# Keeping a third quarter of the expert activations on chip, running the top-k search denser, and loading the gates in smaller pieces behind the weights

## The chip, the cores and the metric

One Trainium2 chip, one core. The metric is device time in microseconds (us) of one execution. The kernel's instructions are spread over TensorE (PE; its weight loads are PEld), VectorE (DVE), ScalarE (ACT), GpSimd (POOL) and SyncE (SP). SP and ACT also issue the transfers between DRAM and SBUF, the on-chip memory; each has its own queue of them (q1 and q10 in the profile).

## The reference, cut to what matters

Two transformer blocks run one after the other on 256 tokens of width 1024. The part that the change touches is the last one, a mixture of 16384 experts (128 x 128) called `peer`. For each token and each of 8 heads, 128 scores on each of two sides give the 16 best of each side, the 16 best of their sums give 16 experts, and a softmax over those gives their gates:

```
s = einsum('thpd,hpnd->thpn', q, sub_keys)
sv, si = top_k(s, 16)
top_v, top_i = top_k(sv0 + sv1 (all pairs), 16);  g = softmax(top_v)
a = gelu(einsum('td,thkd->thk', x, u[experts]))
out = einsum('thk,thkd->td', g * a, v[experts])
```

The kernel does not gather experts. It computes the products with all 16384 rows of `u`, multiplies by a matrix of gates that is zero nearly everywhere, and multiplies that by all of `v`.

## The kernel before, in words

All matrix products are done in about fp32 accuracy: each operand is split in a high and a low part, and each product is three matmuls. `Weights` (L139) brings weights in by tiles `raw` of 128 x 2048 (1 MB, L154, three buffers, issued on SP), and splits each half tile into `whi` (ACT, L133) and `wlo` (DVE, L130), three buffers of each. PE reads only the split halves.

**The u pass** (`u_pass`, L1042). Four quarters q of 32 blocks j; one step takes two blocks, so 16 steps a quarter and 64 in all. A step needs one `raw` tile, does 48 matmuls (L171 to L173) into one PSUM bank and has one Gelu on ACT (L1049). Quarters 0 and 1 go to SBUF tiles `ga[0]` and `ga[1]` and stay. Quarters 2 and 3 go to a ring of four tiles `gr`, and from there to DRAM (`ga_d`, L1051, queue of ACT).

**The side work.** While the u pass runs, a generator makes the gates: first `topk_steps` (L904, 44 pieces; most are the search on DVE; the two halves of the tokens, tt = 0 and 1, each end in transposes on PE, L976), then `g_steps` (L983, 33 pieces). Piece i of the latter builds one-hot matrices for 8 tokens on DVE (L999 to L1002), and does 16 small matmuls of the piece before (L1012), moves their result to a tile `gs` (ACT, L1014) and writes that to DRAM, 512 KB (`gg_d`, L1015, queue of ACT). `feed(n)` (L1029) advances the generator by n pieces on average: one per call in the eight calls of the search's score stage (L898), then 1.2 per step of the u pass while j is below 60 and 1.7 after (L1052). Transposes and gate matmuls are pinned by `issue_after` behind the last matmul traced so far on PE.

**The v pass** (`v_pass`, L1065). Again 64 steps of two blocks, 16 a quarter. A step takes the activations g (from `ga`, or for quarters 2 and 3 read back from DRAM, L1076, queue of SP), multiplies them in place by the gates `gh` (DVE, L1078), splits the product (`wgh` on ACT, `wgl` on DVE, two buffers of each) and does 48/2 = 24 matmuls of 512 columns (L1091). `gh` holds 16 blocks (HJ), 2 MB, two buffers; it is read from `gg_d` in runs of 512 bytes (16 blocks x 8 tokens x 4 bytes) by L1071 on SP's queue, eight times in all.

The order of instructions on each engine and each queue is not the order of the text. A planner lays it down when the kernel is built, from times that it estimates: an instruction that it takes to be ready may come far ahead of its place in the text, if nothing pins it. On the chip each engine then follows its own list in order and waits at each instruction for its operands. The weight loads, the gate loads and the read-backs are all on SP's list.

Of the kernel before, what the change touches and what calls it, by code (L numbers as in the profile page):

```python
# [10 lines left out]
F32 = mybir.dt.float32  # L11
# [5 lines left out]
AF = mybir.ActivationFunctionType  # L17
# [3 lines left out]
P = 128  # L21
S = 256
# [17 lines left out]
NE = NKEYS  # L40
# [23 lines left out]
def block_kernel(ctx: ExitStack, tc: tile.TileContext, a: dict, out: bass.AP, dbg=None):  # L64
    nc = tc.nc

    def pool(stack, name, bufs=1):
        return stack.enter_context(tc.tile_pool(name=name, bufs=bufs, reuse_waits="tile"))
# [8 lines left out]
    def bank(tag, name):  # L77
        return psum.tile([P, 512], F32, tag=tag, bufs=2, name=name)
# [5 lines left out]
    def ps_a(name="psa"):  # L84
        return bank("a", name)

    def ps_b(name="psb"):
        return bank("b", name)

    def ps_c(name="psc"):  # L90
        return bank("c", name)
# [26 lines left out]
    class Lo:  # L118
# [3 lines left out]
        def next(self):  # L122
            self.at += 1
            return self.cycle[self.at % len(self.cycle)]
# [7 lines left out]
    def split(dst_h, dst_l, src, eng="v"):  # L132
        nc.scalar.activation(dst_h, src, AF.Copy)  # L133
        sub(eng, dst_l, src, dst_h)

    last_load = [None]
# [31 lines left out]
    def mm3(ps, w, b, K, xs):  # L168
        for k in range(K):
            wh, wl = w(b + k)  # L170
            nc.tensor.matmul(ps, wh, xs[0][:, k], start=(k == 0), stop=False)  # L171
            nc.tensor.matmul(ps, wh, xs[1][:, k], start=False, stop=False)  # L172
            last_mm[0] = nc.tensor.matmul(ps, wl, xs[0][:, k], start=False, stop=(k == K - 1))  # L173
# [525 lines left out]
    with tc.high_priority():  # L699
# [7 lines left out]
        t = small.tile([P, 2], F32, name="yf2")  # L707
# [95 lines left out]
    for g in range(4):  # L803
        ps = ps_a()
# [46 lines left out]


    QJ = 32
    TG = 8
    NG = S // TG
    big = pool(ctx, "big")
    ga = [big.tile([P, QJ, S], F32, name=f"ga{q}") for q in range(2)]

    ring = pool(ctx, "ring", 4)
    dram = ctx.enter_context(tc.tile_pool(name="dram", bufs=1, space=bass.MemoryType.DRAM))  # L860
    ga_d = [dram.tile([P, QJ // 2, 2 * S], F32, name=f"gad{q}") for q in range(2)]
    gg_d = dram.tile([P, NG, NE * TG], F32, name="ggd")

    idxT = big.tile([P, 2, S], F16, name="idxT")
    gT = big.tile([P, 2, S], F16, name="gT")
# [117 lines left out]
    def g_steps():  # L983

        gp = pool(stg, "gp", 3)
        todo = None
        for i in range(NG + 1):
            new = None
            if i < NG:
                ts = slice(i * TG, (i + 1) * TG)  # L990

                def two(x):
                    return x.rearrange("p (g t) -> p g t", t=2)[:, :, None, :].to_broadcast([P, TG // 2, P, 2])

                io = iota2[:, None].to_broadcast([P, TG // 2, P, 2])
                o1 = gp.tile([P, TG // 2, P, 2], F16, tag="o1", name="o1")
                o2 = gp.tile([P, TG // 2, P, 2], F16, tag="o2", bufs=2, name="o2")
                og = gp.tile([P, 2, TG // 2, P, 2], F16, tag="og", name="og")
                nc.vector.tensor_tensor(o1, io, two(idxT[:, 0, ts]), op=OP.is_equal)  # L999
                nc.vector.tensor_tensor(o2, io, two(idxT[:, 1, ts]), op=OP.is_equal)  # L1000
                for c in range(2):
                    nc.vector.tensor_tensor(og[:, c], o2, two(gT[:, c, ts]), op=OP.mult)  # L1002
                new = i, o1, og
            if todo:
                i_, o1, og = todo
                gs = gp.tile([P, NE, TG], F32, tag="gs", bufs=2, name="gs")
                with tc.issue_after(last_mm[0].ins):
                    for g4 in range(TG // 4):
                        ps = (ps_d, ps_b)[g4]()
                        for t4 in range(4):  # L1010
                            for c in (1, 0):
                                nc.tensor.matmul(ps[:, t4 * P:(t4 + 1) * P], o1[:, 2 * g4 + t4 // 2, :, t4 % 2], og[:, c, 2 * g4 + t4 // 2, :, t4 % 2],  # L1012
                                                 start=(c == 1), stop=(c == 0))
                        nc.scalar.activation(gs[:, :, g4 * 4:g4 * 4 + 4], ps.rearrange("p (t j) -> p j t", t=4), AF.Copy)  # L1014
                nc.scalar.dma_start(gg_d[:, i_], gs.rearrange("p j t -> p (j t)"))  # L1015
            todo = new
            yield

# [2 lines left out]
    def side():  # L1021
        yield from topk_steps()
        st4.close()
        yield from g_steps()
# [4 lines left out]
    def feed(n):  # L1029
        due[0] += n  # L1030
        while due[0] >= 1.0:
            due[0] -= 1.0
            next(side_it, None)
# [8 lines left out]
    def u_pass(q):  # L1042
        w = Weights(a["uT"][:, q * QJ * D:(q + 1) * QJ * D])
        for j in range(0, QJ, 2):
            ps = ps_c()
            for i in range(2):
                mm3(ps[:, i * S:(i + 1) * S], w, (j + i) * KD, KD, h2)
            g = ga[q][:, j:j + 2] if q < 2 else ring.tile([P, 2, S], F32, tag="gr", name="gr")
            nc.scalar.activation(g, ps.rearrange("p (j t) -> p j t", j=2), AF.Gelu)  # L1049
            if q >= 2:  # L1050
                nc.scalar.dma_start(ga_d[q - 2][:, j // 2], g.rearrange("p j t -> p (j t)"))  # L1051
            feed(1.2 if q * QJ + j < 60 else 1.7)  # L1052

    for q in range(4):
        u_pass(q)
    for _ in side_it:
        pass
    stg.close()

    hot = pool(ctx, "hot", 2)  # L1060
    acc = [[ps_a("acc0"), ps_a("acc1")], [ps_b("acc2"), ps_b("acc3")]]

    HJ = 16

    def v_pass(q):  # L1065
        w = Weights(a["v"][:, q * QJ * D:(q + 1) * QJ * D])
        for j in range(0, QJ, 2):
            jj = q * QJ + j
            if j % HJ == 0:
                gh = hot.tile([P, NG, HJ, TG], F32, tag="gh", name="gh")  # L1070
                nc.sync.dma_start(gh, gg_d.rearrange("p g (j t) -> p g j t", t=TG)[:, :, jj:jj + HJ])  # L1071
            if q < 2:
                g = ga[q][:, j:j + 2]
            else:
                g = ring.tile([P, 2, S], F32, tag="gr", name="gr")
                nc.sync.dma_start(g.rearrange("p j t -> p (j t)"), ga_d[q - 2][:, j // 2])  # L1076
            gv = g.rearrange("p j (g t) -> p j g t", t=TG)
            nc.vector.tensor_tensor(gv, gv, gh[:, :, j % HJ:j % HJ + 2].rearrange("p g j t -> p j g t"), op=OP.mult)  # L1078
            wh = hot.tile([P, 2, S], F32R, tag="wgh", name="wgh")
            wl = hot.tile([P, 2, S], F32R, tag="wgl", name="wgl")  # L1080
            split(wh, wl, g)
            end = jj + 2 == NE
            hls = [w((j + i) * KD, KD) for i in range(2)]

            def block(i, tt, ns):
                hi, lo = hls[i]
                first, last = jj + i == 0, jj + i == NE - 1
                th, tl = wh[:, i, tt * P:(tt + 1) * P], wl[:, i, tt * P:(tt + 1) * P]
                for x_, w_, st, sp in ((th, hi, first, False), (th, lo, False, False), (tl, hi, False, last)):
                    for n in ns:  # L1090
                        r = nc.tensor.matmul(acc[tt][n], x_, w_[:, n * 512:(n + 1) * 512], start=st, stop=sp)  # L1091
                return r

            if not end:
                for i, tt in itertools.product(range(2), range(2)):
                    block(i, tt, range(2))
            else:

                r = None
                for tt, n in itertools.product(range(2), range(2)):  # L1100
                    with tc.issue_after(r.ins) if r else nullcontext():
                        for i in range(2):
                            r = block(i, tt, (n,))

    v_pass(0)
    v_pass(1)


# [140 lines left out]
def build(arrays, dbg=None):  # L1249
    import concourse.bacc as bacc  # L1250

    nc = bacc.Bacc("TRN2", target_bir_lowering=False, num_devices=1)
    aps = {n: nc.dram_tensor(f"in_{n}", v.shape, mybir.dt.from_np(v.dtype), kind="ExternalInput").ap()
           for n, v in arrays.items()}
    out = nc.dram_tensor("out_0", (S, D), F32, kind="ExternalOutput").ap()
    taps = None
    if dbg:
        taps = {n: nc.dram_tensor("dbg_" + n, s, F32, kind="ExternalOutput").ap() for n, s in dbg.items()}
    with tile.TileContext(nc, schedule_with_timeline_sim=True) as tc:
        block_kernel(tc, aps, out, taps)  # L1260
    return nc
# [9 lines left out]
```

## Time and profile before

| | us |
|---|---|
| median of 3 runs | 1413.62 (1412.87 to 1416.95) |
| profiled execution, its own time | 1420.62 |
| its span | 1418.8 |
| PE busy | 1375.2 |
| PEld / DVE / ACT / POOL busy | 1270.8 / 1013.1 / 704.9 / 23.8 |

The page is read from the top: busy time of each engine, then the span in 40 slices (35.5 us each) with the clock that TensorE was granted and what the DMA engines moved, then the chain of work that ended last. The queries on the trace used here are the windows (busy time of each engine in a stretch), the waits (who waited for whom), the timeline of one engine, and the view of one line or one tile. In that trace the u pass runs from 636 to about 1057 us and the v pass from there to about 1405 us.

### The profile page before, as it was taken

How to read it: one execution, taken by the hardware profiler on the slowest of the kernel's cores; microseconds unless marked ns; L12 is line 12 of the kernel's file. 1: busy time of each engine (PE TensorE's matmuls, PEld its weight loads, DVE VectorE, ACT ScalarE, POOL GpSimd, SP SyncE). 2: the span in 40 equal slices, each digit the busy share in tenths (PEclk: the TensorE clock that was granted, in tenths of full speed). 3: DMA queues.
4: the chain of work that ended last, by engine and by line, in shares of the span. 5: the costliest groups of instructions: out<-in, count | busy, mean ns of one | idle time of the engine just before them, and what ended most of it. 6: DMA issues, size and time to landing. Idle time of an engine off the chain costs nothing.

```text
span 1418.8 us, 24208 instructions
## 1 busy us (share of the span) xinstructions
PE 1375.2 (97%) x9776; PEld 1270.8 (90%) x9776; DVE 1013.1 (71%) x1749; ACT 704.9 (50%) x1030; POOL 23.8 (2%) x25
## 2 busy tenths in 40 slices
PE   7999999999999999899999999998999999999997
PEld 6967998999999888899999999998888888888885
DVE  6774777998888646699984489876536555566775
ACT  4443654454546555545454456554344454444443
POOL 1000000000000001000000000000000000000000
PEclk9998999999999999999999999999899999999999
DMA  6452456777795632444555578889975555588762
GB/s 239 154 196 82 141 169 234 269 279 267 262 328 191 218 125 72 152 170 158 187 198 180 178 257 311 296 296 321 340 287 197 190 197 199 198 300 289 262 233 86
DMA packets 88448, 308.86 MB, mean 218 GB/s; under 512 B 6416, under 2 KB 39824, under 8 KB 61200
## 3 DMA queue, kind: packets, MB, share of 16 engines
q1 hardware_dynamic: 78544, 279.26, 57.0%
q10 hardware_dynamic: 9792, 28.05, 5.0%
q8 instruction: 76, 1.25, 0.3%
q14 instruction: 36, 0.29, 0.1%
HBM read 281.08 MB, written 26.21 MB: 217 GB/s over the span
## 4 chain that ended last, share of the span: by engine, by line
PE 88%; DVE 5%; DMA 4%; issue 1%; ACT 1%; POOL 0%; SPq 0%; ACTq 0%; POOLq 0%; DVEq 0%
PE acc L1091 24%; PE psa L173 9%; PE psa L171 9%; PE psa L172 9%; PE psc L173 8%; PE psc L171 8%; PE psc L172 8%; DMA aw<-in_ada 2%; PE psb L501 2%; DVE wlo L130 2%; PE psd L1012 1%; PE psb L1012 1%; DMA gh<-ggd 1%; PE psd L771 1%; PE psb L759 1%
## 5 line engine op out<-in xcount | busy, mean ns | idle before, releaser
L133 ACT ACTIVATE whi<-raw 128x1024 fp32r<-128x1024 f32 (+1 forms) x426 | 448.0, 1053 | 502.7 <-PE psa L172 181.6
L130 DVE TENSOR_TENSOR wlo<-raw,whi 128x1024 fp32r<-128x1024 f32 (+1 forms) x426 | 517.4, 1217 | 240.6 <-ACT whi L133 236.9
L171 PE MATMUL psc<-h2h,whi 128*128 128x256 f32 x1024 | 294.3, 288 | 6.4 <-ACT whi L133 6.4
L173 PE MATMUL psc<-h2h,wlo 128*128 128x256 f32 x1024 | 293.8, 288 | 4.2 <-DVE wlo L130 4.2
L172 PE MATMUL psc<-h2l,whi 128*128 128x256 f32 x1024 | 292.7, 286 | 0.0
L171 PEld LDWEIGHTS psc<-h2h,whi 128*128 128x128 f32 x1024 | 199.8, 195 | 7.0 <-ACT whi L133 7.0
L173 PEld LDWEIGHTS psc<-h2h,wlo 128*128 128x128 f32 x1024 | 199.5, 195 | 4.9 <-DVE wlo L130 4.9
L172 PEld LDWEIGHTS psc<-h2l,whi 128*128 128x128 f32 x1024 | 199.8, 195 | 0.0
L1091 PE MATMUL acc<-wlo,wgh 128*128 128x512 f32 x512 | 160.2, 393 | 0.0
L1091 PE MATMUL acc<-whi,wgl 128*128 128x512 f32 x512 | 158.7, 390 | 0.0
L1091 PE MATMUL acc<-whi,wgh 128*128 128x512 f32 x512 | 138.5, 389 | 0.0
L1091 PEld LDWEIGHTS acc<-whi,wgl 128*128 128x128 f32 x512 | 96.1, 188 | 20.2
L1091 PEld LDWEIGHTS acc<-whi,wgh 128*128 128x128 f32 x512 | 96.0, 188 | 20.1
L1091 PEld LDWEIGHTS acc<-wlo,wgh 128*128 128x128 f32 x512 | 94.6, 188 | 19.7
L171 PE MATMUL psa<-acth,whi 128*128 128x256 f32 x352 | 99.9, 284 | 2.0 <-DVE ft L638 1.2
L173 PE MATMUL psa<-acth,wlo 128*128 128x256 f32 x352 | 99.9, 284 | 1.9 <-DVE wlo L130 1.9
L172 PE MATMUL psa<-actl,whi 128*128 128x256 f32 x352 | 99.8, 284 | 0.2 <-DVE actl L293 0.2
L171 PE MATMUL psa<-xh,whi 128*128 128x256 f32 x240 | 71.1, 296 | 8.0 <-ACT whi L133 8.0
L173 PE MATMUL psa<-xh,wlo 128*128 128x256 f32 x240 | 70.4, 293 | 2.6 <-DVE wlo L130 2.6
L172 PE MATMUL psa<-xl,whi 128*128 128x256 f32 x240 | 71.0, 296 | 0.0
L316 DVE SCALAR_TENSOR_TENSOR jk<-aw,row_c 128x1024 bf16<-128x1024 f32 x48 | 58.6, 1220 | 14.8 <-DMA aw<-in_ada 14.4
L171 PEld LDWEIGHTS psa<-acth,whi 128*128 128x128 f32 x352 | 66.9, 190 | 2.6 <-ACT whi L133 1.4
(415 smaller groups left out, 2462.6 us busy)
## 6 DMA issues: line engine op xcount, KB each, us to landing
raw<-in_uT SPq DMA_DIRECT2D x64, 1024.0 KB, 4.9
raw<-in_v SPq DMA_DIRECT2D x64, 1024.0 KB, 4.9
aw<-in_ada SPq DMA_DIRECT2D x48, 512.0 KB, 5.8
raw<-in_wgu SPq DMA_DIRECT2D x22, 1024.0 KB, 4.9
ggd<-gs ACTq DMA_DIRECT2D x32, 512.0 KB, 4.5
gh<-ggd SPq DMA_DIRECT2D x8, 2048.0 KB, 14.3
raw<-in_wA SPq DMA_DIRECT2D x14, 1024.0 KB, 5.0
raw<-in_wdn SPq DMA_DIRECT2D x11, 1024.0 KB, 7.2
```

The lines of the kernel that those rows point to most:

```text
L130: e.tensor_tensor(dst, src, hi.bitcast(F32), op=OP.subtract)
L133: nc.scalar.activation(dst_h, src, AF.Copy)
L171: nc.tensor.matmul(ps, wh, xs[0][:, k], start=(k == 0), stop=False)
L172: nc.tensor.matmul(ps, wh, xs[1][:, k], start=False, stop=False)
L173: last_mm[0] = nc.tensor.matmul(ps, wl, xs[0][:, k], start=False, stop=(k == K - 1))
L316: nc.vector.scalar_tensor_tensor(jk, aw, 1.0, c_, op0=OP.mult, op1=OP.mult, accum_out=dst[:, t:t + 1])
L501: nc.tensor.matmul(s[:, i], q_[:, qb * P:(qb + 1) * P], k_[:, :n], start=(j == 0), stop=False)
L759: nc.tensor.matmul(s, q2[x_][hd, hp, qs_], kall[y_][hd, hp], start=(i == 0), stop=(i == 2))
L771: nc.tensor.matmul(o[:, h * 64:(h + 1) * 64], pts[:, kb * P:(kb + 1) * P], v2[:, kb, h * 64:(h + 1) * 64], start=(kb == 0), stop=(kb == 3))
L1012: nc.tensor.matmul(ps[:, t4 * P:(t4 + 1) * P], o1[:, 2 * g4 + t4 // 2, :, t4 % 2], og[:, c, 2 * g4 + t4 // 2, :, t4 % 2], start=(c == 1), ...
L1091: r = nc.tensor.matmul(acc[tt][n], x_, w_[:, n * 512:(n + 1) * 512], start=st, stop=sp)
```

## The change

Quarter 3 of the activations is kept in SBUF, in a tile `ga3` that is allocated where the tiles of the side work lay, after these are closed; so the u pass is cut into three quarters, the end of the side work, and the last quarter. Only quarter 2 goes through DRAM, and its ring has three tiles. `feed` gives 1.6 pieces per step while j is below 44, then 1.5. The tile `gs` and the pieces of `gg_d` hold 16 tokens (1 MB a write). `gh` holds 8 blocks (1 MB a load, 16 loads; runs of 8 x 16 x 4 = 512 bytes), and each load is pinned on SP behind the last weight load traced before it.

```diff
-    TG = 8
+    TG, TD = 8, 16
-    ring = pool(ctx, "ring", 4)
+    ring = pool(ctx, "ring", 3)
-    ga_d = [dram.tile([P, QJ // 2, 2 * S], F32, name=f"gad{q}") for q in range(2)]
-    gg_d = dram.tile([P, NG, NE * TG], F32, name="ggd")
+    ga_d = dram.tile([P, QJ // 2, 2 * S], F32, name="gad")
+    gg_d = dram.tile([P, S // TD, NE * TD], F32, name="ggd")
...
-                gs = gp.tile([P, NE, TG], F32, tag="gs", bufs=2, name="gs")
+                h = i_ * TG % TD
+                if h == 0:
+                    gs = gp.tile([P, NE, TD], F32, tag="gs", bufs=2, name="gs")
...
-                nc.scalar.dma_start(gg_d[:, i_], gs.rearrange("p j t -> p (j t)"))
+                if h + TG == TD:
+                    nc.scalar.dma_start(gg_d[:, i_ * TG // TD], gs.rearrange("p j t -> p (j t)"))
...
-            g = ga[q][:, j:j + 2] if q < 2 else ring.tile([P, 2, S], F32, tag="gr", name="gr")
+            g = ga[q][:, j:j + 2] if q != 2 else ring.tile([P, 2, S], F32, tag="gr", name="gr")
-            if q >= 2:
-                nc.scalar.dma_start(ga_d[q - 2][:, j // 2], g.rearrange("p j t -> p (j t)"))
-            feed(1.2 if q * QJ + j < 60 else 1.7)
+            if q == 2:
+                nc.scalar.dma_start(ga_d[:, j // 2], g.rearrange("p j t -> p (j t)"))
+            feed(1.6 if q * QJ + j < 44 else 1.5)
-    for q in range(4):
+    for q in range(3):
         u_pass(q)
     for _ in side_it:
         pass
     stg.close()
-
     hot = pool(ctx, "hot", 2)
+    ga += [None, hot.tile([P, QJ, S], F32, bufs=1, name="ga3")]
+    u_pass(3)
...
-    HJ = 16
+    HJ = 8
...
-                gh = hot.tile([P, NG, HJ, TG], F32, tag="gh", name="gh")
-                nc.sync.dma_start(gh, gg_d.rearrange("p g (j t) -> p g j t", t=TG)[:, :, jj:jj + HJ])
-            if q < 2:
+                gh = hot.tile([P, S // TD, HJ, TD], F32, tag="gh", name="gh")
+                with tc.issue_after(last_load[0].ins):
+                    nc.sync.dma_start(gh, gg_d.rearrange("p g (j t) -> p g j t", t=TD)[:, :, jj:jj + HJ])
+            if q != 2:
                 g = ga[q][:, j:j + 2]
             else:
                 g = ring.tile([P, 2, S], F32, tag="gr", name="gr")
-                nc.sync.dma_start(g.rearrange("p j t -> p (j t)"), ga_d[q - 2][:, j // 2])
-            gv = g.rearrange("p j (g t) -> p j g t", t=TG)
+                nc.sync.dma_start(g.rearrange("p j t -> p (j t)"), ga_d[:, j // 2])
+            gv = g.rearrange("p j (g t) -> p j g t", t=TD)
```

## Rows read from the trace of the kernel before

**Rows 1.** The page: busy tenths and granted clock in 40 slices

```profile
PE   7999999999999999899999999998999999999997
...
PEclk9998999999999999999999999999899999999999
```

**Rows 2.** Windows: stretch, length, PE, PEld, DVE, ACT, POOL busy, clock, DMA share, GB/s

```profile
640.00:660.00 20.00, 20.00 (x170) 20.00 (x169) 19.85 (x97) 11.76 (x14) 0.00 (x0) 1.00 0.45 159
760.00:780.00 20.00, 20.00 (x169) 20.00 (x168) 8.46 (x7) 9.19 (x11) 0.00 (x0) 1.00 0.56 203
860.00:880.00 20.00, 20.00 (x218) 19.87 (x217) 19.29 (x28) 12.89 (x21) 0.00 (x0) 1.00 0.86 321
980.00:990.00 10.00, 7.71 (x50) 7.30 (x49) 10.00 (x16) 2.81 (x4) 0.00 (x0) 0.83 1.07 373
1260.00:1280.00 20.00, 20.00 (x90) 16.53 (x89) 13.05 (x15) 10.38 (x12) 0.00 (x0) 1.00 0.91 324
```

**Rows 3.** Waits of PE, 590 to 1418 us: total, times, longest

```profile
PE psc L171 <- ACT whi L133: 6.4, 3, 2.2
PE psc L173 <- DVE wlo L130: 4.2, 3, 2.3
```

**Rows 4.** Timeline of ACT, the Gelu that ends each u step: start, duration

```profile
794.31 0.58 ACT L1049 ACTIVATE ga<-psc 128x512 f32<-128x512 f32 x1
800.07 0.58 ACT L1049 ACTIVATE ga<-psc 128x512 f32<-128x512 f32 x1
...
829.19 0.58 ACT L1049 ACTIVATE gr<-psc 128x512 f32<-128x512 f32 x1
...
1057.68 0.58 ACT L1049 ACTIVATE gr<-psc 128x512 f32<-128x512 f32 x1
```

**Rows 5.** Chain of waits, half of one piece's gate matmuls: start, duration

```profile
838.26 0.46 PE psd L1012 x8
```

**Rows 6.** Timeline of SP, transfers issued at the end of the u pass

```profile
962.60 9.60 SPq L1071 DMA_DIRECT2D gh<-ggd  x2
...
984.83 8.99 SPq L154 DMA_DIRECT2D raw<-in_uT  x1
...
1018.28 0.53 SPq L1071 DMA_DIRECT2D gh<-ggd  x1
```

**Rows 7.** Timelines of ACT and DVE there, with the wait before each

```profile
987.69 2.01 ACT L133 ACTIVATE whi<-raw 128x1024 fp32r<-128x1024 f32 x2 [7.07 <-DMA raw<-in_uT]
...
1008.54 4.90 DVE L1078 TENSOR_TENSOR ga<-ga,gh 128x512 f32<-128x512 f32 x8 [3.08 <-DMA gh<-ggd]
```

**Rows 8.** Timeline of SP in the v pass, around the seventh gate load

```profile
1251.26 0.33 SPq L154 DMA_DIRECT2D raw<-in_v  x1
1252.23 0.54 SPq L1071 DMA_DIRECT2D gh<-ggd  x1
...
1260.73 0.37 SPq L154 DMA_DIRECT2D raw<-in_v  x1
...
1262.14 0.33 SPq L154 DMA_DIRECT2D raw<-in_v  x1
```

**Rows 9.** Tile gh, 1200 to 1418 us: time from issue to landing

```profile
DMA to landing us min/median/max: 11.5/11.8/12.0
```

**Rows 10.** The page: transfers by kind, KB each, median us to landing

```profile
raw<-in_v SPq DMA_DIRECT2D x64, 1024.0 KB, 4.9
...
ggd<-gs ACTq DMA_DIRECT2D x32, 512.0 KB, 4.5
gh<-ggd SPq DMA_DIRECT2D x8, 2048.0 KB, 14.3
```

**Rows 11.** Lines: duration min/median/max ns, first and last start

```profile
L969 DVE TENSOR_TENSOR ix<-eq x4: 273/280/291, 687.1 to 741.6; 128x128 f32<-128x128 f16 x4
...
L976 PE MATMUL psd<-cst,ix x4: 272/272/273, 712.4 to 820.7; 128*128 128x128 f32 x4
```

**Rows 12.** Timeline of DVE, the last sum of the search's first half

```profile
707.06 0.27 DVE L969 TENSOR_TENSOR ix<-eq 128x128 f32<-128x128 f16 x1
```

More of the change, by code (lines that the diff above doesn't have):

```diff
@@ L1013, in g_steps @@
                                                  start=(c == 1), stop=(c == 0))
-                        nc.scalar.activation(gs[:, :, g4 * 4:g4 * 4 + 4], ps.rearrange("p (t j) -> p j t", t=4), AF.Copy)
-                nc.scalar.dma_start(gg_d[:, i_], gs.rearrange("p j t -> p (j t)"))
+                        nc.scalar.activation(gs[:, :, h + g4 * 4:h + g4 * 4 + 4], ps.rearrange("p (t j) -> p j t", t=4), AF.Copy)
+                if h + TG == TD:
+                    nc.scalar.dma_start(gg_d[:, i_ * TG // TD], gs.rearrange("p j t -> p (j t)"))
             todo = new
```

## The prediction

> **What bounds the kernel now.** Read the page's slices first: PE is busy nearly everywhere; of the slices that the change touches (the 17th, at 570 us, and later) two neighbours stand out before the last: the 28th (958 to 993 us) has a busy digit of 8 and the 29th (993 to 1029) a clock digit of 8 [rows 1]. The windows then show what an undisturbed stretch looks like and what this one does: from 760 to 780 us PE is busy for all of the 20 us at clock 1.00, from 980 to 990 us for 7.71 of 10 us at 0.83, with the DMA engines above full share [rows 2]. The waits of PE name only two causes between the start of the u pass and the end: the high half of the weights (6.4 us) and the low half (4.2 us), together 10.6 us in six waits [rows 3]. All of them lie between 980 and 1040 us.
>
> What this stretch costs in all is read from the Gelus, one a step. Two of them lie 5.76 us apart where nothing else runs (794.31 to 800.07) [rows 4]. From the 33rd (829.19) to the 64th (1057.68) there are 31 intervals, 178.6 us at that pace; the 32 pieces of gate matmuls lie in them too, each 2 x 0.46 = 0.93 us on PE [rows 5], 29.7 us. The sum is 208.3 us, the rows give 228.5 [rows 4]: **20.2 us are lost**. [...]
>
> Why: SP's list holds two gate loads of 2 MB right at 962.6 us, as soon as the last gates are written, and four more up to 1018 us, between the weights of the u pass that is not done [rows 6]. A gate load of 2 MB takes 11.5 to 12.0 us to land where only a step's usual traffic runs beside it [rows 9], 14.3 in the median of all [rows 10]; six of them in 60 us are 12 MB beside the weights. SP is held at weight load 984.83 for 8.99 us [rows 6], ACT then waits 7.07 us for weights, and DVE waits 3.08 us for gates and multiplies eight activations in a row (4.90 us) with the weights' low halves behind it [rows 7]. That is the loss. The gates are wanted only from 1057 us on.
>
> **The change part by part.** The sum is made against the profiled execution (1420.6 us, span 1418.8).
>
> *Gate loads pinned behind the weights.* The first load now stands on SP behind the 64th load of u weights, load k behind the weights of step 4k-1 of the v pass. There are three `raw` buffers, and a weight tile's buffer is free when its halves are split, so a weight load is issued some 3.5 steps ahead of PE (an estimate from the buffer counts in the code). The first gates are then asked for some 4 steps of 5.76 us, 23 us, before PE wants them. 1 MB is not in the trace in runs of 512 bytes: no less than the 4.9 us of 1 MB of weights [rows 10], no more than the 12.0 us of 2 MB [rows 9]; I take half of 11.8, 5.9 us, and even 12.0 lies inside 23. The six hoisted loads, 12 MB, leave the u pass but for one or two MB. So the 20.2 us go: -20.2. Bounds: none of it (the planner still lets the multiplies run ahead of the gates on DVE), or all. What is late next? In the undisturbed u steps PE waits for nothing [rows 3] and there is no idle time to win.
>
> *Does a gate load between v weights cost anything?* Before does that twice with 2 MB. After the load of 1252.23 the next weight load is issued at 1260.73 instead of 5.44 us after the one of 1251.26, so 4 us late, and the one after it, 1262.14, is back on pace [rows 8]; PE stays busy for all of 1260 to 1280 us at clock 1.00 [rows 2]. A load of half the size holds SP less. I take 0 for each of the 16. Behind the gate load on SP stand weight loads and read-backs; ACT, then DVE, then PE wait for those, with one to two steps in hand. If that cover were gone, the price would be that of the second rival.
>
> *Quarter 3 in SBUF.* 16 writes and 16 read-backs of 256 KB go, 8 of 309 MB; on PE's path they cost nothing now [rows 3], so 0. `ga3` waits until the side work's tiles are free. By `feed` the 77th and last piece now falls in step 45 (8 + 22 x 1.6 + 23 x 1.5 = 77.7) instead of step 50, and the first Gelu into `ga3` is that of step 49, four steps or 23 us later; the last gate write takes 4.5 us for 512 KB [rows 10], say 9 for 1 MB and 14.3 at worst. Covered: 0; at worst 0 too. The ring of three still gives a write of 256 KB three steps.
>
> *Gates in pieces of 16 tokens.* 16 writes of 1 MB for 32 of 512 KB: the same bytes. Between a write and the next use of its buffer lie three pieces, at 1.5 a step two steps of 5.76 + 1.39 = 7.15 us, so 14.3 us against 9 (bounds 4.5 and 14.3 as above). ACT would wait if it were late, and it is busy 12.89 of 20 us there [rows 2], so a few us of waiting don't reach PE. 0. The evictions (64) and multiplies (64) keep their sizes, only strides change; no row shows the new ones. I take their present durations; they can lie some tenths of a us off either way each, beside idle time of ACT and DVE.
>
> *Denser search.* No instruction is added; their places move. DVE is busy 19.85 of 20 us in the search and 8.46 of 20 after it [rows 2], since the planner already runs it ahead of its place: the last sum is done at 741.6 us, the transposes that wait for their place follow up to 820.7 [rows 11]. The second half's transposes move from step 31 to step 24, which ends near 777 us; 741.6 is before that. The first half's move from step 13 to step 10, which ends near 696 us, while its last sum was done at 707.06 [rows 12]. Either the planner gives the earlier text the earlier slot on DVE, or it puts the transposes behind later matmuls: both 0. [...] The gate pieces then take DVE's free time from 777 us on; at 1.5 a step instead of 1.7 DVE has more room than the 19.29 of 20 us now [rows 2]. PE's work is the same.
>
> Sum: 1420.6 - 20.2 = **1400.4 us for a profiled execution**. The median of the runs is 7.0 us below the profiled one. If those 7.0 lie outside the stall, the new median is 1413.6 - 20.2 = 1393.4; if all lie in it (it is the stretch where DMA is above full share, which a profile would burden most), 1400.4. I take 1396.
>
> [...]
>
> **The rivals.**
>
> 1. *Part of the stall moves to the seam of the passes.* The multiplies of the first gates and the splits of the first products still come into the last u steps on DVE, whose list blocks at a late gate load (3.08 us before eight multiplies [rows 7]). For it: the planner's times for a gate load were short by that much. Against: four multiplies in a row, not eight, and one load in flight. Four late stretches made up the 20.2 us, 5 us each; one or two of them stay: 1396 + 5 to 10 = 1401 to 1406.
>
> 2. *The other side: each gate load in line starves PE.* Place: the weight load behind each of the 16. Price: as in the stall, about 5 us each of idle and slow clock. From four of the 16 on, the gain is eaten; at all 16 it is 1413.6 - 20.2 + 81 = 1474. Against it: rows 8 and 2 with twice the size.
>
> 3. [...]
>
> 4. *It doesn't do what it says.* The multiplies or the read-backs take the gates' place ahead of the weights and the stall stays: 1413.
>
> **How the numbers follow.** Forecast 0.66 (own range 1391 to 1402); first rival 0.17; third 0.06; fourth 0.05; second 0.06. About 4 us, 0.3%, is what a measurement of this kernel can tell from no change. Forecast, first rival and a share of the third are faster by more: 0.85; the fourth and the rest of the third are no change: 0.08; slower 0.07. The range runs from 1388, all 20.2 us gone and then the spread of the runs (4 us) below it, to 1408, a little past the first rival's end.
>
> **What would show it.** Right: on SP no gate load before the last u weight load; Gelus 5.76 us apart from the last gate piece to the end of the u pass; clock 1.00 there; u pass over near 1037 us; 16 gate loads landing in 5 to 8 us, each between two weight loads; last gate matmul near 928 us; transposes near 700 and 777 us with PE never waiting. Wrong: PE waiting for high or low halves at a period of four steps in the v pass (second rival), PE waiting at L976 (third), late Gelus in the last three u steps with DVE waiting at L1078 (first).

## The result, and the profile after

The changed kernel takes 1397.37 us in the median of four runs (1394.19 to 1402.77), against 1415.28 us (1412.87 to 1417.83) for the kernel before: 17.9 us less, ratio 0.988 with a 95% interval of 0.984 to 0.992. On a second chip, in the experiments, it was 1400.02 against 1417.09 us, ratio 0.987 (0.984 to 0.990). The forecast was 1396 us.

The profiled execution of the changed kernel has a span of 1392.4 us, 26.4 us less than before. The page of it, the lines that answer to [rows 1]:

```profile
PE   7999999999999999899999999999999999999997
...
PEclk9998999999999999999999999999999999999999
```

The hole at the 28th and 29th digit is gone. The windows show the same stretches as [rows 2] (columns as there):

```profile
760.00:780.00 20.00, 20.00 (x169) 20.00 (x168) 11.72 (x15) 9.48 (x13) 0.00 (x0) 1.00 0.52 186
860.00:880.00 20.00, 20.00 (x201) 19.87 (x200) 17.18 (x25) 11.71 (x17) 0.00 (x0) 1.00 0.83 307
980.00:990.00 10.00, 10.00 (x85) 10.00 (x85) 4.88 (x4) 4.27 (x6) 0.00 (x0) 1.00 0.53 197
1260.00:1280.00 20.00, 20.00 (x90) 16.54 (x90) 13.47 (x15) 9.49 (x11) 0.00 (x0) 1.00 0.82 294
```

From 980 to 990 us PE is busy for all 10 us at full clock, and the DMA share is half of what it was. From 590 us to the end of its matmuls PE waits for nothing: the two waits of [rows 3] have no counterpart. How long the u pass takes is read from its first and its last Gelu (timeline of ACT; start, duration):

```profile
639.04 0.60 ACT L1052 ACTIVATE ga<-psc 128x512 f32<-128x512 f32 x1
...
1031.87 0.58 ACT L1052 ACTIVATE ga<-psc 128x512 f32<-128x512 f32 x1
```

That is 392.8 us. Before, the first was at 645.63 us and the last at 1057.68 [rows 4], 412.1 us. So the u pass gave 19.2 us. The rest of the span after the last Gelu went from 361.1 to 360.5 us. The other 6.6 us of the 26.4 lie before the first Gelu, where the order of the work is the same; in the second profile of the same changed kernel (below) its first Gelu came at 645.26 us, so these 6.6 us are scatter between executions and no gain. That is also why the medians differ by 18 us and the two spans by 26.

The transfers (timeline of SP) stand in the order that the diff asks for, the first gates behind the last u weights and the next behind four v weights:

```profile
1007.33 0.33 SPq L154 DMA_DIRECT2D raw<-in_uT  x1
1007.75 0.61 SPq L1076 DMA_DIRECT2D gh<-ggd  x1
1013.09 17.61 SPq L154 DMA_DIRECT2D raw<-in_v  x4
1030.79 0.53 SPq L1076 DMA_DIRECT2D gh<-ggd  x1
```

The first gates are asked for 24 us before the last Gelu. They land in 7.9 to 9.4 us, later than the forecast's 5.9, but within its bounds of 4.9 and 12.0. The first line is the tile `gh` (16 loads). The second is the tile `gs`, whose 16 writes don't hold ACT any more (before, ACT waited for them twice, 1.8 us in all).

```profile
DMA to landing us min/median/max: 7.9/8.1/9.4
```

```profile
DMA to landing us min/median/max: 3.9/5.3/9.3
```

On DVE (timeline) the first gates release four multiplies in a row, with no wait before them, where [rows 7] had eight behind a wait of 3.08 us:

```profile
1014.72 1.22 DVE L130 TENSOR_TENSOR wlo<-raw,whi 128x1024 fp32r<-128x1024 f32 x1 [1.66 <-ACT whi L133]
1015.86 2.49 DVE L1083 TENSOR_TENSOR ga<-ga,gh 128x512 f32<-128x512 f32 x4
1018.27 1.22 DVE L130 TENSOR_TENSOR wlo<-raw,whi 128x1024 fp32r<-128x1024 f32 x1
```

### The profile page after: what moved, and what is told of

The parts are those of the page before. It is cut to its first block, busy times and chain, and to the rows that moved or that the text cites. A ratio compares the mean times of both kernels' runs of the same rounds, so it can differ in the third digit from the quotient of the medians.

```text
span 1392.4 us, 24098 instructions
## 1 busy us (share of the span) xinstructions
PE 1362.4 (98%) x9776; PEld 1261.5 (91%) x9776; DVE 1012.3 (73%) x1749; ACT 703.8 (51%) x1030; POOL 23.6 (2%) x25
## 4 chain that ended last, share of the span: by engine, by line
PE 94%; DVE 4%; issue 1%; DMA 1%; ACT 0%; POOL 0%; SPq 0%; POOLq 0%; DVEq 0%; ACTq 0%
PE acc L1096 25%; PE psa L173 10%; PE psa L171 10%; PE psa L172 10%; PE psc L171 9%; PE psc L173 9%; PE psc L172 9%; PE psb L501 2%; DVE wlo L130 1%; PE psd L1014 1%; PE psb L1014 1%; PE psd L771 1%; PE psb L759 1%; PE psd L520 1%; PE psa L204 1%
## 5 line engine op out<-in xcount | busy, mean ns | idle before, releaser
L171 PE MATMUL psc<-h2h,whi 128*128 128x256 f32 x1024 | 291.2, 285 | 0.0
L173 PE MATMUL psc<-h2h,wlo 128*128 128x256 f32 x1024 | 290.0, 284 | 0.0
L172 PE MATMUL psc<-h2l,whi 128*128 128x256 f32 x1024 | 289.8, 283 | 0.0
L172 PEld LDWEIGHTS psc<-h2l,whi 128*128 128x128 f32 x1024 | 196.5, 192 | 0.0
L171 PEld LDWEIGHTS psc<-h2h,whi 128*128 128x128 f32 x1024 | 196.5, 192 | 0.0
L173 PEld LDWEIGHTS psc<-h2h,wlo 128*128 128x128 f32 x1024 | 196.2, 192 | 0.0
L1096 PEld LDWEIGHTS acc<-whi,wgh 128*128 128x128 f32 x512 | 95.9, 188 | 19.9
L173 PEld LDWEIGHTS psa<-acth,wlo 128*128 128x128 f32 x352 | 68.3, 194 | 0.9 <-DVE wlo L130 0.9
```

## The experiments

The times of single kernels scatter by several us, more than half of what some of these edits can be worth. So the measure is taken inside the profiles: U, from the first Gelu of the u pass to the last, and V, from there to the end of the span. U was the same within 0.01 us in three profiles of kernels that don't stall (after, its repeat, and e4). The kernel before was run beside them: its median was 1417.09 us on the chip of after again, e1, e2 and e4, 1414.07 us on that of f1, f2, f3 and e9, and its one run on that of g1, g2, e10 and e8 took 1413.08 us.

| kernel | U, us | V, us | time, us: median, or the one run |
|---|---|---|---|
| before | 412.1 | 361.1 | 1415.28 |
| after | 392.8 | 360.5 | 1397.37 |
| after, again | 392.8 | 360.5 | 1400.02 |
| e1: before, with the pin alone | 396.0 | 366.0 | 1403.79 |
| e2: after, without the pin | 393.7 | 361.9 | 1400.13 |
| e4: after, quarter 3 through DRAM | 392.8 | 360.5 | 1396.28 |
| f1: before, with the pieces alone | 393.7 | 362.1 | 1399.78 |
| f2: before, with the denser feed alone | 413.5 | 361.2 | 1417.27 |
| f3: e4 + six loads of 2 MB, unread | 412.1 | 359.7 | 1411.33 (one run) |
| g1: e4 + five loads of 2 MB, spread, unread | 397.7 | 361.2 | 1405.26 (one run) |
| g2: e4 + twelve loads of 1 MB, unread | 415.1 | 360.5 | 1419.28 (one run) |
| e9: after + four DVE blocks of 4.9 us | 393.3 | 360.0 | 1397.86 (one run) |
| e10: after + four DVE blocks of 8.1 us | 406.6 | 359.5 | 1408.40 (one run) |
| e8: after, gate loads of 512 KB, each twice | 392.8 | 362.7 | 1400.06 (one run) |

**e1, the pin alone.**

```diff
+                with tc.issue_after(last_load[0].ins):
-                nc.sync.dma_start(gh, gg_d.rearrange("p g (j t) -> p g j t", t=TG)[:, :, jj:jj + HJ])
+                    nc.sync.dma_start(gh, gg_d.rearrange("p g (j t) -> p g j t", t=TG)[:, :, jj:jj + HJ])
```

> The kernel before with one edit: its eight gate loads of 2 MB are pinned on SP behind the last weight load traced ahead of them; quarters 2 and 3 still go through DRAM, the feed and the pieces of 8 tokens stay. The measure is the time from the first Gelu of the u pass to its last: 412.1 us before (645.63 to 1057.68), 392.8 after (639.04 to 1031.87). Theory A (the gate loads that came ahead of the u weights are the whole loss): about 393 us, no wait of PE from the u pass on, and a time about 18 us below before, the same as the full change within 4 us. Theory B (the full change needs less traffic too, by quarter 3 in SBUF and earlier gates): 400 us or more, and a time at least 6 us above the full change.

Measured: U 395.99 us, 16.1 of the 19.2 us; V is 4.9 us longer than before and 5.4 us longer than after. Time 1403.79 us (ratio 0.991, 0.987 to 0.995). Theory A had said no waits, and that is not so. The waits of PE, and DVE's timeline at the first two gate loads:

```profile
PE acc L1092 <- DVE wlo L130: 5.0, 3, 2.3
PE psc L173 <- DVE wlo L130: 1.1, 1, 1.1
```

```profile
1021.16 4.91 DVE L1079 TENSOR_TENSOR ga<-ga,gh 128x512 f32<-128x512 f32 x8 [1.63 <-DMA gh<-ggd]
...
1068.68 4.91 DVE L1079 TENSOR_TENSOR ga<-ga,gh 128x512 f32<-128x512 f32 x8 [1.45 <-DMA gh<-ggd]
```

With 2 MB loads DVE waits 1.5 us for the gates and then does eight multiplies before the next low half: it is held for 6.4 to 6.5 us, and PE runs dry: the last two Gelus lie 8.91 us apart instead of 5.76. At the seam of the passes this is the first rival of the prediction. In the v pass the same hold comes back at the next three gate loads (DVE's eight multiplies start at 1068.68, 1113.78 and 1161.92 us), each with one wait of PE; from 1180 us on PE doesn't wait. This is not the second rival, which puts the delay at the weight load behind the gates: ACT waits for no weights there. In the changed kernel all of it is absent.

**e2, everything but the pin.**

```diff
-                with tc.issue_after(last_load[0].ins):
-                    nc.sync.dma_start(gh, gg_d.rearrange("p g (j t) -> p g j t", t=TD)[:, :, jj:jj + HJ])
+                nc.sync.dma_start(gh, gg_d.rearrange("p g (j t) -> p g j t", t=TD)[:, :, jj:jj + HJ])
```

> The full change without the pin on the gate loads; everything else as in it. On SP's list ten of the sixteen 1 MB gate loads then stand ahead of the last u weights again. Theory A: the loss comes back, 405 to 418 us from the first Gelu to the last, PE waits for the split halves of the u weights again, and the time is 10 to 20 us above the full change. Theory B: smaller pieces and less traffic keep most of the gain, under 398 us, and the time is within 5 us of the full change.

Measured: U 393.69 us, 0.9 above the full change, time 1400.13 against 1400.02 us. Theory A fell here. The gate loads are ahead of the weights again (timeline of SP, then the window in which ten of them are issued):

```profile
957.23 0.53 SPq L1075 DMA_DIRECT2D gh<-ggd  x1
...
963.31 0.86 SPq L154 DMA_DIRECT2D raw<-in_uT  x2
964.41 0.53 SPq L1075 DMA_DIRECT2D gh<-ggd  x1
967.76 5.15 SPq L154 DMA_DIRECT2D raw<-in_uT  x1
973.00 0.53 SPq L1075 DMA_DIRECT2D gh<-ggd  x1
```

```profile
934.00:994.00 60.00, 59.39 (x495) 59.19 (x494) 45.22 (x55) 27.69 (x33) 0.00 (x0) 1.00 1.07 350
```

The DMA engines are as full as in the stall of the kernel before, 1.07 of full share, and PE still idles only 0.6 us. So neither that loads are hoisted nor that the engines are full makes the loss by itself.

**The changed kernel again, and e4, quarter 3 through DRAM.**

```diff
-            g = ga[q][:, j:j + 2] if q != 2 else ring.tile([P, 2, S], F32, tag="gr", name="gr")
+            g = ga[q][:, j:j + 2] if q < 2 else ring.tile([P, 2, S], F32, tag="gr", name="gr")
-            if q == 2:
-                nc.scalar.dma_start(ga_d[:, j // 2], g.rearrange("p j t -> p (j t)"))
+            if q >= 2:
+                nc.scalar.dma_start(ga_d[q - 2][:, j // 2], g.rearrange("p j t -> p (j t)"))
```

> The changed kernel itself, on the same chip as the others: 392.8 us from the first Gelu to the last under either theory, and 0.985 to 0.99 of the time before. The first Gelu came 6.6 us earlier than before in its first profile (639.04 against 645.63) although the instructions up to there are the same; if that is scatter from one execution to the next, it differs from 639.0 by some us here.

> The full change with quarter 3 sent through DRAM again (16 writes and 16 reads of 256 KB more), the pin, the denser feed and the pieces of 16 kept. Theory A: 392.8 us from the first Gelu to the last, v pass unchanged, time within 3 us of the full change: quarter 3 in SBUF is worth nothing by itself. Theory B: the 8 MB cost PE waits, 396 us or more, and the time is over 4 us above the full change.

Measured: the first Gelu of the repeat at 645.26 us, as said above. U and V of both kernels are those of the changed kernel to 0.1 us, and no wait of PE. Quarter 3 in SBUF is worth nothing. The median of e4 is lower, 1396.28 us, but its interval (0.981 to 0.988) and the repeat's (0.984 to 0.990) overlap, and no stretch of the two profiles that the edit touches differs; I don't take it for a gain.

**f1, the pieces alone; f2, the feed alone.** With theory A gone, these two ask which part does it by itself. f1 is the kernel before with TD = 16 and HJ = 8, f2 with the new feed.

```diff
-            feed(1.2 if q * QJ + j < 60 else 1.7)
+            feed(1.6 if q * QJ + j < 44 else 1.5)
```

> The kernel before with only the gates in DRAM pieces of 16 tokens and gate loads of 8 blocks (1 MB); no pin, the old feed, quarters 2 and 3 through DRAM, a ring of four. Ten of the sixteen gate loads still stand ahead of the last u weights on SP. The full change without its pin lost only 0.9 us in the u pass (393.69 against 392.83 us from the first Gelu to the last), so theory A, that hoisted loads are the loss whatever their size, has fallen. Theory C (the loss is in the size: 2 MB loads hold SP, and eight multiplies in a row hold DVE): 393 to 396 us here, most of the gain. Theory D (the denser search is what helps, since it writes the gates earlier and spreads the loads over more steps): 400 to 410 us here.

> The kernel before with only the denser feed (1.6, then 1.5). Its 2 MB gate loads are hoisted as before, six of them, but from the 50th u weight load on instead of the 55th. Theory C: the loss stays, 405 us or more from the first Gelu to the last. Theory D: 398 us or less.

Measured: f1 has U 393.67 us and 1399.78 us (ratio 0.988, 0.984 to 0.993); f2 has U 413.50 us and 1417.27 us (ratio 1.002, 0.999 to 1.004). The waits of PE, f1 first and then f2:

```profile
PE psc L173 <- DVE wlo L130: 1.1, 1, 1.1
```

```profile
PE psc L171 <- ACT whi L133: 7.7, 4, 2.4
PE psc L173 <- DVE wlo L130: 5.3, 5, 2.5
```

The pieces alone give 18.4 of the 19.2 us, with ten of the loads still hoisted. They are two edits in one, gate loads of 1 MB instead of 2 and gate writes of 1 MB instead of 512 KB; the two were not run apart. The denser search gives nothing: it moves the stall some 30 us ahead, with the gates.

**f3 and e9, transfers or multiplies.** f3 puts the six transfers of 2 MB back without anything that reads them; e9 puts DVE blocks back without transfers.

```diff
+            for n in range({12: 2, 16: 1, 18: 1, 22: 1, 24: 1}.get(j, 0) if q == 3 else 0):
+                dm = hot.tile([P, 32, 16, 8], F32, tag="dm", name="dm")
+                with tc.issue_after(last_load[0].ins):
+                    nc.sync.dma_start(dm, ...)
```

```diff
+            if q == 3 and j % 8 == 4:
+                dm = small.tile([P, 1], F32, tag="dm", bufs=4, name="dm")
+                with tc.issue_after(last_sub[0].ins):
+                    nc.vector.reduce_sum(dm, ga[0].rearrange("p j t -> p (j t)")[:, :4608], axis=AX.X)
```

> The full change with quarter 3 through DRAM (392.83 us from the first Gelu to the last, no PE wait there), plus six loads of 2 MB from the gates' DRAM in runs of 512 bytes, put on SP where the kernel before had its hoisted gate loads (two behind the 55th u weight load, one each behind the 57th, 58th, 60th and 61st). Nothing reads them, so DVE has no multiplies there. If the transfers are the cause: late weights, PE waits for the high halves, 400 to 412 us. If the multiplies on DVE are the cause: 393 to 395 us.

> The full change plus four sums on DVE over 4608 elements in the last u quarter, each pinned behind a low half of the weights: about 4.9 us each, what eight multiplies in a row took, without any transfer. Their results are not used. If a block of this length holds up the low halves: four late steps, PE waits for the low halves, 2 to 3 us each with the slow clock after it, so 400 to 405 us from the first Gelu to the last. If it takes a late gate load before the multiplies as well (3 us more): 393 to 395 us here.

Measured: f3 has U 412.14 us, within 0.1 us of the kernel before, with not one multiply there. e9 has U 393.34 us: 0.5 us for four blocks, and no wait of PE. ACT's timeline and the waits of PE in f3:

```profile
980.26 2.00 ACT L133 ACTIVATE whi<-raw 128x1024 fp32r<-128x1024 f32 x2 [7.61 <-DMA raw<-in_uT]
```

```profile
PE psc L171 <- ACT whi L133: 9.3, 3, 3.6
PE psc L173 <- DVE wlo L130: 2.3, 3, 0.8
```

So the transfers alone are enough for the whole loss: weights come late (7.61 us here, 7.07 in [rows 7]). It doesn't follow that DVE had no part in the kernel before. The waits are shared out otherwise there (4.2 us for low halves and 6.4 for high ones [rows 3], against 2.3 and 9.3 here), and that U agrees to 0.1 us may be chance.

**g1 and g2, the size of a load or the pace.** Both vary f3. g1 has five loads of 2 MB, one behind every second weight load, and g2 the same bytes as f3 at the same places in loads of 1 MB.

```diff
-            for n in range({12: 2, 16: 1, 18: 1, 22: 1, 24: 1}.get(j, 0) if q == 3 else 0):
+            for n in range({4: 1, 8: 1, 12: 1, 16: 1, 20: 1}.get(j, 0) if q == 3 else 0):
```

```diff
-            for n in range({12: 2, 16: 1, 18: 1, 22: 1, 24: 1}.get(j, 0) if q == 3 else 0):
-                dm = hot.tile([P, 32, 16, 8], F32, tag="dm", name="dm")
+            for n in range({12: 4, 16: 2, 18: 2, 22: 2, 24: 2}.get(j, 0) if q == 3 else 0):
+                dm = hot.tile([P, 16, 8, 16], F32, tag="dm", bufs=4, name="dm")
```

> The full change with quarter 3 through DRAM, plus five loads of 2 MB (runs of 512 bytes) that nothing reads, one behind every second u weight load from the 51st to the 59th: 10 MB of gates beside 10 MB of weights in ten steps, 20 MB in 57.6 us or 347 GB/s, the pace at which ten 1 MB loads cost 0.8 us. Theory E (the pace decides: what is asked for in a stretch against the 340 to 365 GB/s that the DMA engines gave there): 393 to 397 us from the first Gelu to the last. Theory C (the size of one load decides: the next weight load is queued behind 2 MB): 400 to 410 us.

> The full change with quarter 3 through DRAM, plus twelve loads of 1 MB that nothing reads, put in pairs where the six 2 MB loads stood in the run that lost 19 us (four behind the 55th u weight load, two each behind the 57th, 58th, 60th and 61st). Same bytes, same places, half the size. Theory E (pace): 408 to 414 us from the first Gelu to the last, as with the 2 MB loads. Theory C (size): 400 us or less.

Measured: g2 has U 415.11 us, worse than f3 in spite of the smaller loads; theory C falls. g1 has U 397.66 us, 0.7 beyond theory E's range: most of the loss is gone, and some 4 us more is lost than with ten 1 MB loads at that pace (0.8 us, f1), so the size may have a part, a small one. The windows of the stretch with the extra loads, g1 and then g2, and the last line the same for f1:

```profile
940.00:1015.00 75.00, 71.60 (x587) 70.48 (x587) 29.44 (x25) 31.37 (x37) 0.00 (x0) 1.00 1.06 353
```

```profile
960.00:1040.00 80.00, 67.82 (x493) 65.90 (x492) 25.18 (x21) 26.36 (x31) 0.00 (x0) 0.90 1.08 345
```

```profile
960.00:1022.00 62.00, 60.86 (x505) 60.46 (x505) 45.72 (x55) 28.32 (x33) 0.00 (x0) 1.00 1.04 349
```

All three move about the same, 345 to 353 GB/s; over the stalls of before (962 to 1040 us), f3 and f2 it is 334, 339 and 325. What differs more is how much of it is weights. In g2, as in the kernel before, 12 MB of gates are asked for beside the seven u weight loads from the 55th to the 61st: 19 loads of 1024 KB (1.05 million bytes) in seven steps of 5.76 us, 19.9 million bytes in 40.3 us, 494 GB/s. In f1 it is one gate load per weight load, 2.1 million bytes in 5.76 us, 364 GB/s, a little above the pace given, and it loses a little. (g1 asks for the same; the 347 of its expectation counts in MB of 1024 KB.) So where the pace asked is far above the pace given, the gates come out of the weights. All loads of gates here are in runs of 512 bytes; no run held the bytes and varied the run length in this stretch.

**e10, a longer DVE block; e8, the gate loads in line made heavier.** e10 is e9 with 7680 elements. e8 has HJ = 4 and this:

```diff
+                    for _ in range(1):
+                        dm = hot.tile([P, S // TD, HJ, TD], F32, tag="dm", name="dm")
+                        nc.sync.dma_start(dm, gg_d.rearrange("p g (j t) -> p g j t", t=TD)[:, :, jj:jj + HJ])
```

> The full change plus four sums on DVE over 7680 elements in the last u quarter, about 8 us each, without any transfer: what DVE is held for when it waits some 3 us for a gate load of 2 MB and then does its eight multiplies. Blocks of 4.9 us cost 0.5 us in all. By the three buffers of split weights a hold of 8 us should be past the cover: four late steps of 2 to 4 us and PE waits for the low halves, 400 to 408 us from the first Gelu to the last. If the cover is longer, 393 to 395 us.

> The full change with gate loads of 4 blocks (512 KB, runs of 256 bytes, 32 of them) and each of them followed by a second one that nothing reads: in the v pass twice the bytes of gates and four times the pieces, in line with the weights. The v pass of the full change took 360.5 us from the last Gelu to the end with no wait of PE. By the second rival, that gate loads in line starve PE, this must show it if anything does: weights and gates are then 2 MB + 1 MB in 10.9 us, 290 GB/s, and more engine time if short runs cost more. Expected: 360 to 380 us; 360.5 still, if short runs cost the DMA engines little; over 400 if they cost double.

Measured: e10 has U 406.63 us, 13.8 us for four blocks, 3.45 each. The block on DVE, and the waits of PE:

```profile
L1060 DVE TENSOR_REDUCE dm<-ga x4: 8146/8147/8147, 951.1 to 1031.1; 128x1 f32<-128x7680 f32 x4
```

```profile
PE psc L172 <- ACT ga L1053: 3.8, 3, 1.3
PE psc L174 <- DVE wlo L130: 2.7, 4, 0.8
PE psc L268 <- ACT ga L1053: 1.3, 1, 1.3
```

So the cover (three split buffers, by the code) ends between a hold of 4.9 us, which costs 0.1 us, and one of 8.1 us, which costs 3.45; e1's hold of 6.5 us at the seam already costs 3.15. In the kernel before DVE was held twice for about as long as in e10 (7.7 and 8.0 us), by a wait for gates and the eight multiplies behind it, once as in [rows 7] and once here:

```profile
976.42 4.90 DVE L1078 TENSOR_TENSOR ga<-ga,gh 128x512 f32<-128x512 f32 x8 [2.84 <-DMA gh<-ggd]
```

By e10 such holds would cost PE time without any late weights; by f3 they add little, if anything, to a stall that is there already. The change meets both causes.

e8 has V 362.68 us: 2.2 us more, with one wait of PE for a high half (1.3 us), for twice the bytes and four times the pieces in line, with the DMA engines above full share for much of the pass (window of e8):

```profile
1200.00:1300.00 100.00, 100.00 (x443) 82.81 (x442) 68.08 (x74) 48.66 (x56) 0.00 (x0) 1.00 1.10 316
```

## Why the prediction was right, and where its step was wrong

- **The size and place of the loss** were right: 19.2 us in the u pass against 20.2. The 1.0 us is the term of the gate matmuls: in the changed kernel the 20 intervals that hold the 32 pieces add up to 145.9 us, 30.7 above 20 x 5.76, so 0.96 us a piece and not the 0.93 worked out from [rows 5]. With 10.6 us of idle time [rows 3], 8.6 us of the 19.2 are left for matmuls at the slow clock, where 20.2 would leave 9.6. In the trace of before the granted clock was 0.50 from 983.3 to 986.5 us, behind a wait of 2.29 us, and 0.50 again from 993.7 to 996.7 us, behind one of 1.97 us.
- **The step "Gate loads pinned behind the weights: -20.2"** gave the whole gain to the pin. The mechanism behind it, transfers ahead of need that make weights late, was right (f3 has the whole loss without a multiply). The attribution was not: without the pin the gain stays (e2), and the pieces alone give 18.4 of 19.2 us (f1). The pin alone gives 16.1 us and makes the v pass 4.9 us longer than before (e1). Either edit cures the pace; only the pieces cure the hold of DVE as well.
- **The order of the waits** was misread: that SP is held at 984.83 us for 8.99 us, and ACT "then" waits 7.07 us. ACT's wait ended at 987.69 us, before that hold did. The weights that it waited for were issued at 972.25 us, right behind the first two gate loads, and took 15.4 us to land (timeline of SP, then L154 from 972 to 976 us):

```profile
972.25 8.10 SPq L154 DMA_DIRECT2D raw<-in_uT  x2
```

```profile
DMA to landing us min/median/max: 15.4/15.4/15.4
```

- **The step "Gates in pieces of 16 tokens: 0"** weighed the writes and the strides, and passed over the change of `HJ` with it. That halves what two buffers can ask for before DVE must free one (by the code), and halves the multiplies that one landing releases (four instead of eight, above). These are the 18.4 us of f1 that the sum gave to the pin.
- **Quarter 3 in SBUF, 0, and the denser search, 0**: both right (e4, f2).
- **The third rival**, that the denser search stalls PE at the transposes of the search's first half, did not come. The last sum of the search's first half is done at 699.8 us, 11 us after the transposes' new place, and the planner put that one transpose behind later matmuls (its result is moved at 704.11 us); PE did not wait.
- **The second rival** did not come. What stood behind a gate load was held up: in the kernel before SP is held for 7.79 us at the read-back right behind the 2 MB load of [rows 8], and in f3 ACT waits 7.61 us for weights that stand behind gate loads. But in line with the v weights this has no price (V is 360.5 us, and PE doesn't wait), and e8 needs twice the bytes in four times the pieces to lose 2.2 us.

```profile
1252.83 7.79 SPq L1076 DMA_DIRECT2D gr<-gad  x1
```

- **The first rival** is what the pin alone gives (e1), and what pieces of 8 blocks remove.
- **Profile against runs**: the 7.0 us between the profiled execution and the median before were split between two ends. The part of the span before the first Gelu, which no edit touches, ended between 637.7 and 645.6 us in the profiles; scatter of this size was there, and was no part of the stall. That a profile burdens a stretch full of transfers most was the author's estimate, and no run shows it; the first profile of the changed kernel took 1394.19 us, less than the median of its runs. So 1396 was a choice between 1393.4 and 1400.4, and that the median came out 1.4 us from it is luck, with four runs from 1394.19 to 1402.77 us.

Left open: what the 4 us are that g1 loses beyond f1, since nothing was run with the size varied at that pace and all else held; what the 1 MB loads give without the 1 MB writes; whether the pace is one of bytes or of runs; and what sets the scatter ahead of the u pass.

## What to carry to other kernels

Loads hoisted ahead of their need were nearly free here up to about the pace that the DMA engines gave in that stretch (345 to 353 GB/s; ten loads of 1 MB at 364 GB/s asked cost 0.8 us), and far beyond it (494 GB/s asked; 22.3 us lost in g2) they came out of the loads that were needed now: add up what is asked for per step and compare, before looking for a place to pin it. With two buffers, halving the load halved both what could be asked for ahead (by the code) and the block of work that a landing released on the engine behind it (four multiplies, 2.49 us, for eight, 4.90 us). Where a change has several parts, run each alone and each left out: here two parts each cured most of the same loss, and two did nothing.

## What was not expected of the hardware

1 MB of gates in runs of 512 bytes took 8.1 us to land, where 1 MB of weights takes 4.9 [rows 10]. This is not the gates' own time: it counts from the issue, and the first gate load is issued at 1007.75 us, 0.42 us behind a weight load on the same queue. The two move one after the other, the weights (runs of 8 KB by the code) first and then the gates: from 1010 to 1011 us the DMA queue of SP shows 52 packets, none under 8 KB, and from 1012 to 1014 us 1240, all under 2 KB. These are the windows of the two stretches; the last line is from e8, where 1 MB of gates in runs of 256 bytes moves:

```profile
1010.00:1011.00 1.00, 1.00 (x10) 1.00 (x10) 0.18 (x1) 0.26 (x1) 0.00 (x0) 1.00 1.01 426
1012.00:1014.00 2.00, 2.00 (x19) 2.00 (x18) 1.06 (x1) 0.38 (x1) 0.00 (x0) 1.00 1.15 317
```

```profile
1208.00:1212.00 4.00, 4.00 (x20) 3.30 (x18) 3.58 (x5) 1.78 (x3) 0.00 (x0) 1.00 1.41 244
```

So the weights moved at 426 GB/s, gates in runs of 512 bytes at 317, and in runs of 256 bytes at 244, with the DMA engines full in all three (shares of 1.01, 1.15 and 1.41). The pace that a stretch gave went with what was in it: 12 MB of gates at 317 and 7 MB of weights at 426 would be 350 GB/s together (an estimate from these windows), and g2 moved 345; 10 us of the stall before moved 373 GB/s [rows 2].
